# S5 input and output turned between channel order and (step, channel) order by DMA through DRAM instead of by quarter copies and column-strip products

## The chip, the cores and the metric

The kernel runs on one core of one Trainium2 chip. The metric is the device time of one execution in microseconds (us), lower is better. TensorE is called PE here, VectorE DVE, ScalarE ACT, GpSimd POOL and SyncE SP, as in the profile.

## What is computed

One decoder layer on a sequence of 512 steps and 1024 channels: a SwiGLU FFN, a token mixer, a second SwiGLU FFN, each with modulation from a vector c, a scaled residual and a LayerNorm. The mixer projects its input once; one half of the result feeds a Mamba-2 (SSD) head group, the other 512 channels, `u`, an S5 head group, and one output projection joins both. The S5 half is what the change touches:

```python
def s5_mixer(u, ...):
    uf = u.reshape(bsz, s_len, S5_GROUPS, S5_GROUP_CH)          # 32 groups of 16 channels
    bu_re = einsum('bsgh,gph->bsgp', uf, bb_re)                 # 64 complex states per group
    bu_im = einsum('bsgh,gph->bsgp', uf, bb_im)
    _, _, xr, xi = lax.associative_scan(combine, (a_seq_re, a_seq_im, bu_re, bu_im), axis=1)
    y = (einsum('bsgp,ghp->bsgh', xr, c_re) - einsum('bsgp,ghp->bsgh', xi, c_im) + uf * d)
    g = gelu(y)
    out = g * sigmoid(g @ w_glu + b_glu)
```

## The kernel before

The whole layer is written as one program. A scheduling layer takes the instructions in the order in which the code issues them and sets each engine's order from its own costs; an engine then runs its own list strictly in order, and a semaphore wait at its head holds all behind it. Large matrix products are done in three passes (high by high, high by low, low by high: lines 103, 104 and 105, `mm3`), so each weight tile is cast to a high part on ACT (`whi`, line 96) and its low part is subtracted on DVE (`wlo`, line 81).

The S5 half works on four blocks b of 128 channels. The scan runs over 128 groups of four steps: a column of the operand U holds four consecutive steps of 32 channels in its 128 partitions, that is (step, channel) order, and four such operands (r = 0 to 3) make a block. The input projection delivers channel order: 128 channels in the partitions, 512 steps along them. So the data has to be turned twice, before the scan and after it.

- `s5_u` (lines 930 to 940) turns the input: `u()` runs a projection of 24 matmuls, then 16 copies of 32 partitions x 128 steps from PSUM into U, 12 of them on ACT (line 938) and 4 on DVE (line 940).
- `s5_scan` (line 942) multiplies U by two matrices (line 949, 8 products per block), and on DVE rotates the result by E (line 81), scans its real and imaginary part (line 960) and rotates back into two tiles `s5X` (line 81 again). `s5_load` (line 927) loads the matrices of a block, `s5M`, from a DRAM buffer that an earlier phase filled.
- `s5_y` (line 970) multiplies U and the two X by three more matrices (line 978): 48 products per block, each 32 columns wide, four of them side by side in the four column strips, which write channel order straight into PSUM; one ACT copy (line 980) moves it to G.
- `s5_glu` (line 983) applies Gelu in place (line 993), splits G into a high and a low part (`ghl`) and multiplies by w_glu.

`mixer` (line 1247) issues these steps mixed with the conv projections of the SSD half, `conv`, also 24 matmuls each followed by ACT line 1111, three DVE passes of line 90 (`cv`) and a Silu (line 1115). The order is u(0), u(1), scan(0), u(2), scan(1), u(3), conv(4), y(0), conv(6), scan(2), conv(5), conv(7), y(1), conv(0), scan(3), y(2), conv(1), conv(2), y(3), the first part of the glu, conv(3), then the SSD scores (lines 1123 to 1134). The scheduler may shift them against one another. Every scan gets X tiles of its own from a pool with one buffer, so a scan's first X write waits until the y before it has read.

Of the kernel before, what the change touches and what calls it, by code (L numbers as in the profile page):

```python
# [10 lines left out]
F32 = mybir.dt.float32  # L11
# [3 lines left out]
AF = mybir.ActivationFunctionType  # L15
# [35 lines left out]
class Layer:  # L51
# [875 lines left out]
        self.nc.sync.dma_start(out=M, in_=self.s5_dram[b][:, k0:k0 + n])  # L927
        return M

    def s5_u(self, U, ups):  # L930

        nc = self.nc
        uv = ups.rearrange("p (t i) -> p i t", i=4)
        for r in range(4):
            for ii in range(4):
                o, a = U[32 * ii:32 * ii + 32, r, :], uv[32 * r:32 * r + 32, ii, :]
                if (r + ii) % 4 < 3:
                    nc.scalar.copy(out=o, in_=a)
                else:
                    nc.vector.tensor_copy(o, a)  # L940

    def s5_scan(self, sp, b, M, U):

        nc = self.nc
        w = []
        for n in range(2):
            ps = self.bank([P, 4, P])
            for r in range(4):
                nc.tensor.matmul(ps[:, r, :], M[:, n, r, :], U[:, r, :], start=True, stop=True)  # L949
            w.append(ps)  # L950
        mk = lambda n: sp.tile([P, 4, P], F32, tag="s5" + n, bufs=1, name=self.nm("s5" + n))
        d0, vr, vi = mk("d0"), mk("vr"), mk("vi")
        t = self.tmp.tile([P, 512], F32, tag="t2", name=self.nm("s5t")).rearrange("p (r t) -> p r t", r=4)
        nc.scalar.copy(out=d0, in_=bc(self.s5_m4[:, 4 * b:4 * b + 4], (2, P)))
        nc.gpsimd.memset(d0[:, :, 0:1], 0.0)
        Er, Ei = M[:, 2], M[:, 3]
        self.cmul(vr, vi, Er, Ei, w[0], w[1], None, t, conj=True)
# [3 lines left out]
        X = [sp.tile([P, 4, P], F32, tag=f"s5X{n}", bufs=1, name=self.nm("s5X")) for n in range(2)]  # L961
        for x in X:
            nc.gpsimd.memset(x[:, :, 0:1], 0.0)
        s = slice(0, P - 1)
        self.cmul(X[0][:, :, 1:], X[1][:, :, 1:], Er[:, :, s], Ei[:, :, s], vr[:, :, s], vi[:, :, s],
                  None, t[:, :, s])
        return X

    def s5_y(self, M, U, X, G):


        nc = self.nc
        ps = self.bank()
        pv = ps.rearrange("p (t j) -> p j t", j=4)
        for j in range(4):
            for n, rhs in enumerate((U, X[0], X[1])):
                for r in range(4):
                    nc.tensor.matmul(pv[32 * r:32 * r + 32, j, :], M[:, n, r, 32 * j:32 * j + 32],  # L978
                                     rhs[:, r, :], start=(n == 0), stop=(n == 2))
        return nc.scalar.copy(out=G, in_=ps).ins  # L980

    def s5_glu(self, G, mixT, after):


        nc = self.nc
        gl = []

        def split(k):
            gl.append(self.tmp.tile([P, 2, S], F32R, tag="t4", name=self.nm("ghl")))
            self.split(G[k], gl[k][:, 0, :], gl[k][:, 1, :])  # L990
        with self.tc.issue_after(after):
            for k in range(4):
                nc.scalar.activation(G[k], G[k], AF.Gelu_apprx_tanh)
        split(0), split(1)
# [253 lines left out]
    def mixer(self, hT, hp, job, finish):  # L1248
# [3 lines left out]
        with ExitStack() as ctx:  # L1252
# [33 lines left out]
            with tc.tile_pool(name="s5", bufs=1, reuse_waits="tile") as sp:  # L1286
# [5 lines left out]

                def u():
                    U.append(Ub[len(U)])
                    self.s5_u(U[-1], proj())

                def scan():
                    b = len(X)
# [1 line left out]
                    load(0)  # L1300

                def y(b):
                    i = self.s5_y(M[1][b], U[b], X[b], G[b])
                    load(1)
                    return i
                load(0), load(0), load(1), load(1)
# [17 lines left out]
                conv(1)  # L1324
                conv(2)
                mixT = []
                glu = self.s5_glu(G, mixT, y(3))
# [103 lines left out]
def body(tc, ins, out):  # L1431
# [3 lines left out]
    with ExitStack() as ctx:  # L1435
# [89 lines left out]
        L.pin = False  # L1525
        L.setup_cols()
        L.s5_m4 = L.cp.tile([P, 16], F32, name="s5m4")
        L.s5_dram = [tc.dram_tile([P, 7, 4, P], F32, name=f"s5d{b}") for b in range(4)]
        gp = gctx.enter_context(tile_pool("g1"))
        L.accp = gp  # L1530
# [118 lines left out]
```

## Time and profile before

| | |
|---|---|
| median of 3 runs | 968.11 us (967.95 to 968.97) |
| the profiled execution, its own time | 968.27 us |
| its span, first to last instruction | 966.6 us |
| PE, busy share of the span | 98% |
| DVE | 78% |
| ACT | 46% |
| DMA, mean over the span | 153 GB/s |

The profile is of one execution, and 1.7 us of its time lie outside its span. Busy time says how long an engine had an instruction in flight; matmuls are pipelined, one 512-column matmul shows 0.39 us but the next starts 0.227 us later. The granted TensorE clock is given as a share of 2.4 GHz: 1.00 is 2.4, 0.50 is 1.2.

### The profile page before, as it was taken

What the parts mean: (1) busy time and instruction counts of PE and PEld (TensorE: products, weight loads), DVE (VectorE), ACT (ScalarE), POOL (GpSimd) and SP (SyncE); (2) the same over time, 40 slices, a digit from 0 to 9 for tenths busy, and PEclk for the clock granted to TensorE, in tenths of its full rate; (3) what the DMA queues carried; (4) which work ended last, traced back from release to release, by engine and by line L of the source; (5) the groups of instructions that cost most, each with busy time, mean ns of one, the idle gap of its engine ahead of it and who ended that gap; (6) DMA issues with size and microseconds to landing.
All of it is one profiled execution on the core that took longest, in us unless ns stands there. A gap on an engine that the chain in (4) does not pass through costs nothing.

```text
span 966.6 us, 14710 instructions
## 1 busy us (share of the span) xinstructions
PE 944.9 (98%) x5409; PEld 798.1 (83%) x5409; DVE 758.4 (78%) x1522; ACT 446.9 (46%) x879; POOL 34.2 (4%) x73
## 2 busy tenths in 40 slices
PE   8999999999999999999999999999999999999996
PEld 5778888887877888778877777988999999988885
DVE  6579998963677888858995889785788888896947
ACT  3343452635443335545537844533455554633420
POOL 0000000000000000100000110100000000000003
PEclk9999999999999999999999999999999999999999
DMA  9968584453866766362432024532233232543302
GB/s 342 377 190 270 188 280 162 157 174 122 261 204 197 242 217 180 86 233 71 142 121 67 1 88 152 173 111 66 88 99 120 89 129 90 175 152 109 109 1 87
DMA packets 75578, 147.93 MB, mean 153 GB/s; under 512 B 11633, under 2 KB 28657, under 8 KB 74993
## 3 DMA queue, kind: packets, MB, share of 16 engines
q1 hardware_dynamic: 75216, 146.94, 46.1%
q8 instruction: 42, 0.69, 0.3%
q14 instruction: 32, 0.25, 0.1%
q10 hardware_dynamic: 288, 0.04, 0.0%
HBM read 137.52 MB, written 9.44 MB: 152 GB/s over the span
## 4 chain that ended last, share of the span: by engine, by line
PE 86%; DVE 6%; ACT 4%; issue 2%; POOL 1%; DMA 0%; DVEq 0%; POOLq 0%; ACTq 0%
PE ps L103 27%; PE ps L104 27%; PE ps L105 27%; DVE cv L90 1%; PE ps L253 1%; PE ps L978 1%; DVE wlo L81 1%; PE ps L207 1%; ACT whi L96 1%; POOL rsx L170 1%; DVE s5X L81 0%; DMA raw<-in_w_in_dram 0%; PE ps L295 0%; DVE s5t L81 0%; PE ps L949 0%
## 5 line engine op out<-in xcount | busy, mean ns | idle before, releaser
L96 ACT CAST whi<-raw 128x1024 fp32r<-128x1024 f32 (+1 forms) x155 | 155.0, 1007 | 211.5 <-PE ps L104 97.5
L81 DVE TENSOR_TENSOR wlo<-raw,whi 128x1024 fp32r<-128x1024 f32 (+1 forms) x155 | 179.3, 1167 | 43.0 <-ACT whi L96 42.5
L103 PE MATMUL ps<-hT,whi 128*128 128x512 f32 x448 | 177.0, 396 | 1.7 <-ACT hT L1492 1.7
L104 PE MATMUL ps<-hT,whi 128*128 128x512 f32 x448 | 174.7, 390 | 0.1
L105 PE MATMUL ps<-hT,wlo 128*128 128x512 f32 x448 | 174.6, 390 | 0.0
L103 PE MATMUL ps<-whi,ghl 128*128 128x512 f32 x320 | 125.2, 391 | 0.0
L104 PE MATMUL ps<-wlo,ghl 128*128 128x512 f32 x320 | 124.5, 389 | 0.0
L105 PE MATMUL ps<-whi,ghl 128*128 128x512 f32 x320 | 124.3, 389 | 0.0
L103 PEld LDWEIGHTS ps<-hT,whi 128*128 128x128 f32 x448 | 83.9, 188 | 23.3 <-issue 3.2
L105 PEld LDWEIGHTS ps<-hT,wlo 128*128 128x128 f32 x448 | 84.1, 188 | 17.8
L104 PEld LDWEIGHTS ps<-hT,whi 128*128 128x128 f32 x448 | 84.2, 188 | 17.0 <-DVE hT L81 0.5
L103 PE MATMUL ps<-hx,whi 128*128 128x256 f32 (+1 forms) x320 | 97.5, 305 | 0.7 <-DVE cp L90 0.6
L104 PE MATMUL ps<-hx,whi 128*128 128x256 f32 (+1 forms) x320 | 97.3, 304 | 0.0
L105 PE MATMUL ps<-hx,wlo 128*128 128x256 f32 (+1 forms) x320 | 97.3, 304 | 0.0
L90 DVE SCALAR_TENSOR_TENSOR acc<-ra,cs,acc 128x1024 f32<-128x1024 f32 (+2 forms) x62 | 71.0, 1145 | 22.4 <-DMA ra<-in_w_ada_dram 21.9
L96 ACT CAST ghl<-g 128x512 fp32r<-128x512 f32 x88 | 53.1, 619 | 50.1 <-PE ps L105 37.5
L103 PEld LDWEIGHTS ps<-whi,ghl 128*128 128x128 f32 x320 | 60.1, 188 | 14.6 <-issue 2.5
L105 PEld LDWEIGHTS ps<-whi,ghl 128*128 128x128 f32 x320 | 60.1, 188 | 12.6
L104 PEld LDWEIGHTS ps<-wlo,ghl 128*128 128x128 f32 x320 | 60.1, 188 | 12.3
L81 DVE TENSOR_TENSOR ghl<-g,ghl 128x512 fp32r<-128x512 f32 x88 | 58.1, 686 | 13.6 <-ACT ghl L96 13.6
L103 PEld LDWEIGHTS ps<-hx,whi 128*128 128x128 f32 x320 | 61.1, 191 | 3.9 <-issue 0.8
L104 PEld LDWEIGHTS ps<-hx,whi 128*128 128x128 f32 x320 | 61.2, 191 | 2.6
(474 smaller groups left out, 1693.0 us busy)
## 6 DMA issues: line engine op xcount, KB each, us to landing
ra<-in_w_ada_dram SPq DMA_DIRECT2D x56, 512.0 KB, 4.5
raw<-in_up_dram SPq DMA_DIRECT2D x49, 512.0 KB, 4.2
raw<-in_ffn_w_dram SPq DMA_DIRECT2D x44, 512.0 KB, 4.4
raw<-in_up_dram SPq DMA_DIRECT2D x64, 256.0 KB, 3.8
ra<-in_ada_dram SPq DMA_DIRECT2D x16, 512.0 KB, 7.8
raw<-in_w_in_dram SPq DMA_DIRECT2D x16, 512.0 KB, 4.4
s5d<-s5mp SPq DMA_DIRECT2D x20, 256.0 KB, 3.8
s5M<-s5d SPq DMA_DIRECT2D x4, 1024.0 KB, 5.1
```

Source lines behind the costliest of these rows:

```text
L81: self.nc.vector.tensor_tensor(out=out, in0=a, in1=b, op=op)
L90: self.nc.vector.scalar_tensor_tensor(out=out, in0=a, scalar=s, in1=b, op0=op0, op1=op1, **k)
L96: keep(self.nc.scalar.copy(out=hi, in_=src))
L103: mm(o, lh, rh, start=first, stop=False, **k)
L104: mm(o, lh, rl, start=False, stop=False, **k)
L105: self.last_mm = mm(o, ll, rh, start=False, stop=last, **k)
L170: self.nc.gpsimd.tensor_scalar(out=x, in0=var, scalar1=EPS, scalar2=None, op0=ADD)
L207: self.nc.tensor.matmul(ps, self.onesr, bc(self.onesr, (1, 4)), start=True, stop=True)
L253: nc.tensor.matmul(bank[q:q + 32, 0:256], lhs, w[:, :, m * P:(m + 1) * P], start=(j < 2), stop=(j >= len(put) - 2))
L978: nc.tensor.matmul(pv[32 * r:32 * r + 32, j, :], M[:, n, r, 32 * j:32 * j + 32], rhs[:, r, :], start=(n == 0), stop=(n == 2))
```

## The change

It turns both ways by DMA. `s5_turn` takes a channel-order tile of 128 partitions, issues four writes of 64 KB each into a DRAM buffer on ACT's DMA queue, in 512-byte pieces that land in (step, channel) order or back, and then one read of the whole 256 KB on POOL's queue. The input takes one ACT copy from PSUM and one turn. The output is now 12 full-width products per block in (step, channel) order, one ACT copy, and one turn whose result overwrites the block's U; Gelu reads that and writes G with a stride. The two X tiles and the decay row d0 are allocated and their first columns cleared once, for all four scans; the ACT copy of a scan fills the rest of d0.

```diff
+    def s5_turn(self, b, n, src, out):
+        d = self.s5_turns[b][:, n]
         for r in range(4):
-            for ii in range(4):
-                o, a = U[32 * ii:32 * ii + 32, r, :], uv[32 * r:32 * r + 32, ii, :]
-                if (r + ii) % 4 < 3:
-                    nc.scalar.copy(out=o, in_=a)
-                else:
-                    nc.vector.tensor_copy(o, a)
+            self.nc.scalar.dma_start(out=d[:, r].rearrange("(j c) t -> c j t", j=4), in_=src[32 * r:32 * r + 32])
+        self.nc.gpsimd.dma_start(out=out, in_=d)
+    def s5_u(self, b, U, ups):
+        c = self.tmp.tile([P, 1024], F32, tag="t4", ...)[:, :512].rearrange("p (j t) -> p j t", j=4)
+        self.nc.scalar.copy(out=c, in_=ups.rearrange("p (t i) -> p i t", i=4))
+        self.s5_turn(b, 0, c, U)
...
-        d0, vr, vi = mk("d0"), mk("vr"), mk("vi")
+        if b == 0:
+            self.s5_d0, *self.s5_x = mk("d0"), mk("X0"), mk("X1")
+            for a in (self.s5_d0, *self.s5_x):
+                nc.gpsimd.memset(a[:, :, 0:1], 0.0)
+        d0, X = self.s5_d0, self.s5_x
-        nc.scalar.copy(out=d0, in_=bc(self.s5_m4[:, 4 * b:4 * b + 4], (2, P)))
-        nc.gpsimd.memset(d0[:, :, 0:1], 0.0)
+        nc.scalar.copy(out=d0[:, :, 1:], in_=bc(self.s5_m4[:, 4 * b:4 * b + 4], (2, P - 1)))
-        X = [sp.tile([P, 4, P], F32, tag=f"s5X{n}", bufs=1, ...) for n in range(2)]
-        for x in X:
-            nc.gpsimd.memset(x[:, :, 0:1], 0.0)
...
+    def s5_y(self, b, M, U, X, G):
-        for j in range(4):
+        for r in range(4):
             for n, rhs in enumerate((U, X[0], X[1])):
-                for r in range(4):
-                    nc.tensor.matmul(pv[32 * r:32 * r + 32, j, :], M[:, n, r, 32 * j:32 * j + 32],
-                                     rhs[:, r, :], start=(n == 0), stop=(n == 2))
-        return nc.scalar.copy(out=G, in_=ps).ins
+                nc.tensor.matmul(ps[:, r, :], M[:, n, r, :], rhs[:, r, :], start=(n == 0), stop=(n == 2))
+        c = self.tmp.tile([P, 1024], F32, tag="t4", ...)[:, :512].rearrange("p (j t) -> p j t", j=4)
+        i = nc.scalar.copy(out=c, in_=ps).ins
+        self.s5_turn(b, 1, c, G)
+        return i
+    def s5_glu(self, T, G, mixT, after):
-                nc.scalar.activation(G[k], G[k], AF.Gelu_apprx_tanh)
+                nc.scalar.activation(G[k].rearrange("p (t j) -> p j t", j=4), T[k], AF.Gelu_apprx_tanh)
```

Three places show how the engines' lists move. The changed file has two lines more from line 930 on, so its line 977 is the product of line 978, its 950 that of 949, its 1116 that of 1115.

The first is PE's list at y(0). `ps_4627` is its bank, `zx` holds U, `s5X_4418` and `s5X_4419` are the X of block 0; the X of block 1 are two other tiles. Before:

```order
L1080 MATMUL ps_4618<-ident,nacs 32x128
L978 MATMUL ps_4627<-zx_4225,s5M_4233 32x128 x4
L978 MATMUL ps_4627<-s5X_4418,s5M_4233 32x128 x4
L978 MATMUL ps_4627<-s5X_4419,s5M_4233 32x128 x4
L978 MATMUL ps_4627<-zx_4225,s5M_4233 32x128 x4
```

Now, with one pair of X tiles for all blocks:

```order
L977 MATMUL ps_4589<-zx_4229,s5M_4237 128x128
L977 MATMUL ps_4589<-s5X_4391,s5M_4237 128x128
L103 MATMUL ps_4617<-hT_2999,whi_4342 128x512
L977 MATMUL ps_4589<-s5X_4392,s5M_4237 128x128
L977 MATMUL ps_4589<-zx_4229,s5M_4237 128x128
```

The code issues y(0) behind scan(1), and as both now name the tiles s5X_4391 and s5X_4392, y(0) takes them as scan(1) leaves them; in the same way y(1) stands behind scan(2), and y(2) and y(3) behind scan(3). In the list of before, y(0) waits for scan(0) alone.

The second is PE's list from scan(3) on. `ps_4837` is the bank of y(2), `ps_4931` that of y(3), `ps_4809` and `ps_4814` those of scan(3). Before, all of y(2) followed scan(3) at once. Now:

```order
L950 MATMUL ps_4809<-zx_4229,s5M_4494 128x128 x4
L950 MATMUL ps_4814<-zx_4229,s5M_4494 128x128 x4
L977 MATMUL ps_4837<-zx_4229,s5M_4609 128x128
...
L977 MATMUL ps_4837<-s5X_4391,s5M_4609 128x128
...
L977 MATMUL ps_4931<-zx_4229,s5M_4770 128x128
L977 MATMUL ps_4931<-s5X_4391,s5M_4770 128x128
...
L977 MATMUL ps_4837<-s5X_4392,s5M_4609 128x128
L977 MATMUL ps_4837<-zx_4229,s5M_4609 128x128
L977 MATMUL ps_4837<-s5X_4391,s5M_4609 128x128
L977 MATMUL ps_4837<-s5X_4392,s5M_4609 128x128
```

The first gap holds 44 matmuls of conv(1) and conv(2), the second and third four each, of conv(2) and conv(3); the rest of y(2) and then of y(3) follow without a gap, and 20 matmuls of conv(3) behind them.

The third is ACT's list from y(2) to the glu. `s5c_4850` and `s5c_4944` are the copies of y(2) and y(3), `s5t` the DRAM buffers, `zx_4229` holds the turned blocks, `zx_4226` G. Before, the list read (the copy of y(2), line 980, stands further ahead):

```order
L980 COPY zx_4222<-ps_5071 128x512
L993 ACT_TABLE_LOAD
L993 ACTIVATE zx_4222<-zx_4222 128x512
L1115 ACT_TABLE_LOAD
L1115 ACTIVATE zx_4223<-cv_5065 128x512
L993 ACT_TABLE_LOAD
L993 ACTIVATE zx_4222<-zx_4222 128x512 x3
```

Now:

```order
L979 COPY s5c_4850<-ps_4837 128x512
L934 DMA s5t_645<-s5c_4850 32x4x128 x4
L1116 ACTIVATE zx_4227<-cv_4925 128x512
L979 COPY s5c_4944<-ps_4931 128x512
L994 ACT_TABLE_LOAD
L994 ACTIVATE zx_4226<-zx_4229 128x4x128
L934 DMA s5t_646<-s5c_4944 32x4x128 x4
L994 ACTIVATE zx_4226<-zx_4229 128x4x128 x2
L96 CAST ghl_4955<-zx_4226 128x512
```

Two table loads are gone; eight DMA issues stand ahead of the first `ghl`, and so does the Gelu of block 2, which needs that block's turn.

## Rows read from the trace of the kernel before

**Rows 1.** The page's busy time of two engines: busy us, share of the span, instructions.
```profile
PE 944.9 (98%) x5409; PEld 798.1 (83%) x5409; DVE 758.4 (78%) x1522; ACT 446.9 (46%) x879; POOL 34.2 (4%) x73
```

**Rows 2.** Busy time in two stretches of 20 us in the S5 stage; the columns are the stretch, its length, then busy time and instructions of PE, its weight loads, DVE, ACT and POOL, the granted PE clock, the DMA engines' busy share and GB/s.
```profile
440.00:460.00 20.00, 20.00 (x108) 17.21 (x107) 19.30 (x38) 11.18 (x35) 0.10 (x1) 1.00 0.25 79
...
480.00:500.00 20.00, 17.68 (x244) 14.99 (x244) 20.00 (x28) 8.37 (x12) 0.38 (x5) 0.91 0.42 145
```

**Rows 3.** PE in order of time around y(0) and y(2): start, us, line, operation, in brackets the idle time before it and what ended it. A block's y has 96 records (48 products in two passes each).
```profile
460.83 0.43 PE L978 MATMUL ps<-zx,s5M 128*32 128x128 f32 x8
463.59 0.50 PE L103 MATMUL ps<-hT,whi 128*128 128x512 f32 x1
...
492.82 0.43 PE L978 MATMUL ps<-s5X,s5M 128*32 128x128 f32 x8 [0.24 <-DVE s5X L81]
495.33 0.65 PE L978 MATMUL ps<-s5X,s5M 128*32 128x128 f32 x8 [2.08 <-DVE s5X L81]
...
499.23 0.50 PE L103 MATMUL ps<-hT,whi 128*128 128x512 f32 x1
```

**Rows 4.** A stretch of 1 us right behind that wait, in the columns of rows 2.
```profile
496.00:497.00 1.00, 1.00 (x24) 1.00 (x20) 1.00 (x2) 1.00 (x2) 0.00 (x0) 0.50 0.51 195
```

**Rows 5.** PE in order of time at two other places with waits.
```profile
397.51 0.50 PE L103 MATMUL ps<-zw,hT 128*128 128x512 f32 x1 [0.74 <-ACT hT L96]
...
399.39 0.62 PE L105 MATMUL ps<-zw,hT 128*128 128x512 f32 x1 [1.14 <-DVE hT L81]
...
434.33 0.41 PE L1029 MATMUL ps<-ident,dtfm 16*128 16x16 f32 x4 [0.80 <-ACT dtfm L1026]
```

**Rows 6.** DVE in order of time: one input copy of 16; then without a gap a weight split, a product, the scan and another product; the first product of scan(2); a conv pass and the last X write of scan(3).
```profile
443.64 0.28 DVE L940 COPY zx<-ps 32x128 f32<-32x128 f32 x1
...
457.94 1.22 DVE L81 TENSOR_TENSOR wlo<-raw,whi 128x1024 fp32r<-128x1024 f32 x1
459.07 0.68 DVE L81 TENSOR_TENSOR s5t<-s5M,ps 128x512 f32<-128x512 f32 x1
459.67 1.22 DVE L960 TENSOR_TENSOR_SCAN s5vr<-s5d,s5vr 128x512 f32<-128x512 f32 x1
460.81 0.67 DVE L81 TENSOR_TENSOR s5vi<-s5vi,s5t 128x512 f32<-128x512 f32 x1
...
475.96 0.67 DVE L81 TENSOR_TENSOR s5vr<-s5M,ps 128x512 f32<-128x512 f32 x1
...
508.96 0.74 DVE L90 SCALAR_TENSOR_TENSOR cv<-ps,cols,cv 128x511 f32<-128x511 f32 x1
509.62 0.68 DVE L81 TENSOR_TENSOR s5X<-s5X,s5t 128x508 f32<-128x508 f32 x1
```

**Rows 7.** PE in order of time: the products of scan(0), the conv or projection matmul behind them, the products of scan(1).
```profile
440.26 1.95 PE L949 MATMUL ps<-zx,s5M 128*128 128x128 f32 x16
441.96 0.48 PE L103 MATMUL ps<-hT,whi 128*128 128x512 f32 x1
...
447.86 2.03 PE L949 MATMUL ps<-zx,s5M 128*128 128x128 f32 x16
```

**Rows 8.** ACT in order of time: the first input copies of block 0 and of block 1.
```profile
430.58 0.78 ACT L938 COPY zx<-ps 32x128 f32<-32x128 f32 x3
...
441.30 0.79 ACT L938 COPY zx<-ps 32x128 f32<-32x128 f32 x3
```

**Rows 9.** The second of the two issues that ACT's DMA queue had, at the start of the program: start, us, line.
```profile
1.22 0.46 ACTq L188 DMA_DIRECT2D b_ada<-in_badaT_dram  x1
```

**Rows 10.** DMA issues of 256 KB on SP's queue, the first kind out of DRAM, the second into it: count, KB each, median us from issue to landing.
```profile
raw<-in_up_dram SPq DMA_DIRECT2D x64, 256.0 KB, 3.8
...
s5d<-Er SPq DMA_DIRECT2D x4, 256.0 KB, 2.5
```

**Rows 11.** The spread over all transfers into and out of the S5 buffer in DRAM.
```profile
DMA to landing us min/median/max: 2.0/4.2/10.6
```

**Rows 12.** Two stretches in which the first turn would run, in the columns of rows 2.
```profile
430.00:432.00 2.00, 2.00 (x11) 0.77 (x9) 1.26 (x2) 1.34 (x4) 0.00 (x0) 1.00 1.01 422
...
436.00:438.00 2.00, 2.00 (x11) 1.65 (x10) 0.26 (x2) 1.65 (x3) 0.00 (x0) 1.00 0.01 2
```

**Rows 13.** ACT in order of time, from the copy of y(3) to the first split of the glu.
```profile
513.24 0.59 ACT L980 COPY zx<-ps 128x512 f32<-128x512 f32 x1
513.85 1.28 ACT L993 ACT_TABLE_LOAD   x1
515.14 0.63 ACT L993 ACTIVATE zx<-zx 128x512 f32<-128x512 f32 x1
...
520.59 1.12 ACT L96 CAST ghl<-zx 128x512 fp32r<-128x512 f32 x2
```

**Rows 14.** PE in order of time: y(3), the last matmul of conv(3), the SSD scores, the glu.
```profile
510.35 0.42 PE L978 MATMUL ps<-zx,s5M 128*32 128x128 f32 x8
...
518.45 0.39 PE L105 MATMUL ps<-hT,wlo 128*128 128x512 f32 x1
518.68 0.38 PE L1123 MATMUL ps<-zx 128*128 128x128 f32 x2
...
521.25 1.21 PE L103 MATMUL ps<-ghl,whi 128*128 128x512 f32 x4 [0.35 <-ACT ghl L96]
```

**Rows 15.** A stretch of 40 us behind the glu, in the columns of rows 2.
```profile
560.00:600.00 40.00, 37.32 (x180) 30.33 (x181) 34.86 (x53) 17.04 (x38) 3.96 (x8) 1.00 0.39 134
```

More of the change, by code (lines that the diff above doesn't have):

```diff
@@ L928, in s5_load @@
         return M
-    def s5_u(self, U, ups):
-        nc = self.nc
-        uv = ups.rearrange("p (t i) -> p i t", i=4)
+    def s5_turn(self, b, n, src, out):
+        d = self.s5_turns[b][:, n]
         for r in range(4):
-            for ii in range(4):
-                o, a = U[32 * ii:32 * ii + 32, r, :], uv[32 * r:32 * r + 32, ii, :]
-                if (r + ii) % 4 < 3:
-                    nc.scalar.copy(out=o, in_=a)
-                else:
-                    nc.vector.tensor_copy(o, a)
+            self.nc.scalar.dma_start(out=d[:, r].rearrange("(j c) t -> c j t", j=4), in_=src[32 * r:32 * r + 32])
+        self.nc.gpsimd.dma_start(out=out, in_=d)
+    def s5_u(self, b, U, ups):
+        c = self.tmp.tile([P, 1024], F32, tag="t4", name=self.nm("s5c"))[:, :512].rearrange("p (j t) -> p j t", j=4)
+        self.nc.scalar.copy(out=c, in_=ups.rearrange("p (t i) -> p i t", i=4))
+        self.s5_turn(b, 0, c, U)
     def s5_scan(self, sp, b, M, U):
@@ L951, in s5_scan @@
         mk = lambda n: sp.tile([P, 4, P], F32, tag="s5" + n, bufs=1, name=self.nm("s5" + n))
-        d0, vr, vi = mk("d0"), mk("vr"), mk("vi")
+        if b == 0:
[3 more added lines that the diff above has]
+        d0, X = self.s5_d0, self.s5_x
+        vr, vi = mk("vr"), mk("vi")
         t = self.tmp.tile([P, 512], F32, tag="t2", name=self.nm("s5t")).rearrange("p (r t) -> p r t", r=4)
-        nc.scalar.copy(out=d0, in_=bc(self.s5_m4[:, 4 * b:4 * b + 4], (2, P)))
-        nc.gpsimd.memset(d0[:, :, 0:1], 0.0)
+        nc.scalar.copy(out=d0[:, :, 1:], in_=bc(self.s5_m4[:, 4 * b:4 * b + 4], (2, P - 1)))
         Er, Ei = M[:, 2], M[:, 3]
@@ L960, in s5_scan @@
             nc.vector.tensor_tensor_scan(out=fl(v), data0=fl(d0), data1=fl(v), initial=0.0, op0=MUL, op1=ADD)
-        X = [sp.tile([P, 4, P], F32, tag=f"s5X{n}", bufs=1, name=self.nm("s5X")) for n in range(2)]
-        for x in X:
-            nc.gpsimd.memset(x[:, :, 0:1], 0.0)
         s = slice(0, P - 1)
@@ L967, in s5_scan @@
         return X
-    def s5_y(self, M, U, X, G):
+    def s5_y(self, b, M, U, X, G):
         nc = self.nc
-        ps = self.bank()
-        pv = ps.rearrange("p (t j) -> p j t", j=4)
-        for j in range(4):
+        ps = self.bank([P, 4, P])
+        for r in range(4):
             for n, rhs in enumerate((U, X[0], X[1])):
-                for r in range(4):
-                    nc.tensor.matmul(pv[32 * r:32 * r + 32, j, :], M[:, n, r, 32 * j:32 * j + 32],
-                                     rhs[:, r, :], start=(n == 0), stop=(n == 2))
-        return nc.scalar.copy(out=G, in_=ps).ins
-    def s5_glu(self, G, mixT, after):
+                nc.tensor.matmul(ps[:, r, :], M[:, n, r, :], rhs[:, r, :], start=(n == 0), stop=(n == 2))
+        c = self.tmp.tile([P, 1024], F32, tag="t4", name=self.nm("s5c"))[:, :512].rearrange("p (j t) -> p j t", j=4)
+        i = nc.scalar.copy(out=c, in_=ps).ins
+        self.s5_turn(b, 1, c, G)
+        return i
+    def s5_glu(self, T, G, mixT, after):
         nc = self.nc
@@ L1294, in u @@
                     U.append(Ub[len(U)])
-                    self.s5_u(U[-1], proj())
+                    self.s5_u(len(U) - 1, U[-1], proj())
                 def scan():
@@ L1302, in y @@
                 def y(b):
-                    i = self.s5_y(M[1][b], U[b], X[b], G[b])
+                    i = self.s5_y(b, M[1][b], U[b], X[b], U[b])
                     load(1)
@@ L1326, in mixer @@
                 mixT = []
-                glu = self.s5_glu(G, mixT, y(3))
+                glu = self.s5_glu(U, G, mixT, y(3))
                 next(glu)
@@ L1527, in body @@
         L.s5_m4 = L.cp.tile([P, 16], F32, name="s5m4")
+        L.s5_turns = [tc.dram_tile([P, 2, 4, P], F32, name=f"s5t{b}") for b in range(4)]
         L.s5_dram = [tc.dram_tile([P, 7, 4, P], F32, name=f"s5d{b}") for b in range(4)]
```

## The prediction, made blind

> **What bounds the kernel now.** I read the page's busy table first: PE is busy 98% of the span [rows 1], so the change can move the end only by what it does to PE's own work and to PE's waits. Then the table by stage. In the S5 stage DVE is nearly as full as PE, 19.3 and 20.0 of 20 us in two of its stretches [rows 2]: it is DVE's list that PE waits for. PE in order of time shows the one large wait. At y(2) PE stands 0.24 and then 2.08 us for DVE's last X writes, and behind that the granted clock is 0.50, the lower level of 1.2 GHz [rows 3, 4]. The 80 records from 495.33 to 499.23 take 3.9 us; y(0) does 96 in 2.76 us, so 80 are worth 2.3, and 1.6 us went to the clock. This place costs 2.3 + 1.6 = 3.9 us. A second, smaller wait of 0.35 us stands before the glu [rows 14].
>
> The clock has a second witness: waits of 0.74 and 1.14 us, two matmuls between them, are followed by matmuls of 0.62 instead of 0.39 us, while one wait of 0.80 us leaves the next ones alone [rows 5].
>
> **The change, part by part.** *Copies.* 48 small ACT copies and 16 on DVE go. On DVE one takes 0.28 us [rows 6] and some 0.32 with the gap behind it; eleven of them stand between the first product of scan(0) and the last X write at 510.3, 3.5 us of a full engine.
>
> *Products of y.* The 16 records of scan(0) take 441.96 - 440.26 = 1.70 us at full width [rows 7]. The 24 full-width records of a y take 1.5 times that, 2.55 us, against 2.76 [rows 3]. That is 0.2 us a block, 0.8 at most in four.
>
> *The turn of the input.* ACT's copy of 128x512 takes 0.59 us [rows 13] and starts where the copies started, 430.58 and 441.30 [rows 8]. Four issues follow at 0.46 us [rows 9], so the last begins 0.6 + 3 x 0.46 = 2.0 us after the copy's start. A 256 KB write into DRAM lands in 2.5 us and a read of 256 KB in 3.8 [rows 10]; no issue of POOL's queue is in the trace, and I take the read's row for it. That is 2.0 + 2.5 + 3.8 = 8.3 us a turn. The bounds are 2.0 us for each half, the fastest transfer, and 10.6 for a half in full engines, the slowest [rows 11]: 6.0 to some 15 us. With 8.3 us U(0) is there at 438.9, or a little later, since the engines are full with the `s5M` loads at 431 (share 1.01) [rows 12]; PE wants it at 440.26 [rows 7]. U(1) is there at 449.6 and PE wants it at 447.86 [rows 7]: a new wait of 1.7 us. U(2) and U(3) have 10 us and more to spare. Behind the four issues, from 433.0 on, ACT has the copy `dtfm`, which PE waits for up to 434.33 as it is [rows 5]; I cost that at nothing.
>
> On this a rule speaks against the change. The Trainium skill, DMA: Bandwidth & Descriptors, section Anatomy of one DMA, says that a DMA costs about 2 us however small it is, most of it for the confirmation that the last byte has landed, worst when the target is HBM. By it, with 0.6 us for the 256 KB at its 436 GB/s, an estimate for a turn is 2.0 + 2.0 + 2.6 = 6.6 us, and U(1) would be there at 447.9 with no wait; the rows say 8.3, and this trace has no pair of dependent transfers to decide it.
>
> *The new wait of y(0).* It now reads X as scan(1) leaves it, so it waits for DVE's whole list up to there. DVE's `wlo` follows the cast that ACT ends at 441.3, when its copies begin [rows 8], and takes 1.13 us [rows 6]. From there the list of the changed kernel holds 24 products of scan(0) and scan(1) at 0.60 us start to start, four scans of 1.14, two splits of 1.13 and a short `dec` of 0.1 [rows 6]. That is 442.5 + 14.4 + 4.6 + 2.3 + 0.1 = 463.9; with some gaps where a product needs the one before, 464.2. U(0) may be 0.9 us late for PE, and U(1) 3.0 us, before this list moves. PE comes to y(0) at 460.8 [rows 3], or at 462.5 after a wait for U(1). So PE loses about 3 us between 447 and 464, in one portion or two. Ten products are left after 464.2, 2.1 us: y(0) ends at 466.4. If the clock drops as it did at y(2), 1.6 us more, 468.0. Before, y(0) and the one matmul that now stands inside it ended at 463.8. So PE is 2.6 to 4.2 us late here.
>
> *Where that goes.* Scan(2) follows 22 matmuls later; its first bank is ready 5.0 + 1.0 us after y(0), at 472.4 to 474.0, and DVE, which has one `bd`, three conv passes, three short ones and a split in between, some 6.5 us, is free by 470.7 and starts it then instead of at 475.96 [rows 6]. ACT's casts of `csel` hold its second product, as they do before; I allow them up to 0.9 us in the early case. From there DVE's list is as long as before, 34.3 us to the last X write at 510.3 [rows 6]. It ends at 507.5 to 508.5, 1.8 to 2.8 us sooner. PE meets y(1) without a wait of weight, and y(2) no longer stalls: only its first product stands behind scan(3), the rest after 44 matmuls. The 3.9 us of rows 3 and 4 are what pays for the wait at y(0).
>
> *The end of the stage.* Call the last X write T. Before, PE starts y(3) at T and the glu at 521.25, T + 10.9 [rows 14]. Now 19 products of y(2) and y(3), 4.05 us, 20 matmuls of 0.23 [rows 14], 4.55, and the scores, 521.25 - 0.35 - 518.68 = 2.2 [rows 14], make T + 10.8. But ACT's list is longer: its Silu of conv(2) waits for DVE's two splits of 1.13 and four conv passes of 0.66 [rows 6], to T + 5.0; then Silu 0.65, copy 0.65, table load 1.3, Gelu 0.65, four issues 1.8, two Gelus 1.3, split 0.55 [rows 9, 13]: T + 11.9. So the glu begins 1.0 us after PE is ready. The turn of y(2) (copy at T + 2.3, 8.3 us) lands at T + 10.6, just where its Gelu stands; each us more is a us of delay. POOL holds its read behind two clears that wait for y(3), to T + 5.3, which is earlier than the writes land.
>
> *Sum.* 2.8 or 1.8 sooner at T, less 1.0 at the glu: 1.8 or 0.8 us gained. After the glu PE has 2.7 us of waits between 560 and 600 [rows 15], and I let them stand. I take 1.0 us, the middle less a little for a late turn. Against its own 968.27 that is 967.3; the runs' median is 968.11, 0.2 lower, so the forecast is 967.1.
>
> **Rivals.** *Faster: the waits stay short.* If the turn takes 6 to 7 us and PE's 3 us of waiting are split between scan(1) and y(0) with work between, the clock stays up (0.80 us alone did not drop it, rows 5), T is at 507.5, the Gelus come sooner, and the two saved table loads shorten ACT's list behind the glu. Then the gain is up to 2.8: 965.3 to 966.1. Against it: the two cases that did drop the clock had 1.9 and 2.3 us of waiting, and here are about 3.
>
> *Slower: the turn is on the path.* U(0) is needed on DVE by 441.2 and U(1) by 450.9. Beyond that, DVE's list up to y(0) moves one for one, and the turn of y(2) delays the glu one for one as well. The point is a turn of about 9.5 to 10 us. At 13 us (a read of 8.5, between the median and the slowest) U(0) comes 2.4 us late for DVE and U(1) 3.4, and the turn of y(2) costs 4.7 at the glu: 968.1 - 1.0 + 3.4 + 4.7 = 975 at worst, 970 to 972 for 11 us. For it: POOL's queue is unmeasured, 512-byte pieces are small, and the engines are full at 431. Against it: they are empty from 436 and the median rows give 8.3.
>
> *Nothing moves.* The copies were hidden on ACT, half idle, and what DVE saves is eaten by the later X that y(0) reads: within 0.2% with another cause than mine, the same time.
>
> **From cases to numbers.** 0.2% (1.9 us) is about what a measurement of this kernel tells from no change. The forecast, with a gain or a loss below it, 0.5 including the last rival; the faster rival 0.26; the slower one 0.24. The range leaves out half of the outer two: 965.2 to 970.9. The forecast's own range is 966.2 to 969.
>
> **What would show it.** Right: an idle entry of 1 to 2 us before the products of scan(1), ended by a DMA; PE waiting for s5X at y(0) and, with the first, some 3 us in all; no wait at y(1) and y(2); a wait of about 1 us for `ghl` at the glu; DVE some 4.5 us less busy, ACT some 13. Wrong: a turn above 10 us or below 7 from the copy's start to the read's landing; the granted clock at 1.00 all through the S5 stage (then the gain is larger); a Gelu of block 2 waiting for its DMA; PE's waits after the glu grown or shrunk by more than 1 us.

## The result: slower by half a per cent

| | before | changed |
|---|---|---|
| median of 6 runs | 968.03 us (966.54 to 968.97) | 973.91 us (971.29 to 975.56) |
| ratio, 95% interval | | 1.0055, 1.0039 to 1.0071 |
| profiled execution, own time and span | 968.27, 966.6 | 971.4, 969.7 |

The forecast was 967.1 us in a range of 965.2 to 970.9. The change is 5.9 us slower, outside that range, and clear of 0.2%.

The page of the changed kernel, answering to [rows 1]. DVE has 5.7 us less work and ACT 10.6 us less, as the change promises; PE is no busier. The loss is in PE's waits.

```profile
PE 942.5 (97%) x5121; PEld 796.8 (82%) x5121; DVE 752.7 (78%) x1506; ACT 436.3 (45%) x833; POOL 36.0 (4%) x72
```

PE of the changed kernel in order of time, the rows with a wait from 430 to 522, in the columns of [rows 3] (they answer to [rows 3, 5, 7, 14]):

```profile
431.96 0.42 PE L1030 MATMUL ps<-ident,dtfm 16*128 16x16 f32 x4 [0.67 <-ACT dtfm L1027]
439.88 2.05 PE L950 MATMUL ps<-zx,s5M 128*128 128x128 f32 x16 [1.84 <-DMA zx<-s5t]
448.06 2.02 PE L950 MATMUL ps<-zx,s5M 128*128 128x128 f32 x16 [0.27 <-PE ps L1062]
462.01 0.46 PE L977 MATMUL ps<-s5X,s5M 128*128 128x128 f32 x2 [0.65 <-DVE s5X L81]
463.45 0.46 PE L977 MATMUL ps<-s5X,s5M 128*128 128x128 f32 x2 [0.76 <-DVE s5X L81]
504.40 0.49 PE L977 MATMUL ps<-s5X,s5M 128*128 128x128 f32 x2 [0.36 <-DVE s5X L81]
521.19 1.94 PE L103 MATMUL ps<-ghl,whi 128*128 128x512 f32 x4 [2.89 <-ACT ghl L96]
```

The stall at y(2) is gone, as forecast. New are 1.84 us for the turn of block 0 at scan(0), 1.41 us at y(0), and 2.89 us at the glu. The clock fell there too, where [rows 4] show it at y(2):

```profile
522.00:524.00 2.00, 2.00 (x6) 1.54 (x5) 2.00 (x4) 2.00 (x3) 0.00 (x0) 0.50 0.00 0
```

Where the time went can be cut at matmuls that both profiles have: the `dtfm` transposes, the first product of the glu, and the first and the last product of the second FFN's first tiles (`hx,wg`).

| stretch, us | before | changed | difference |
|---|---|---|---|
| start to the `dtfm` transposes | 434.33 | 431.96 | -2.37 |
| to the glu | 86.92 | 89.23 | +2.31 |
| to the first `hx,wg` | 84.52 | 86.73 | +2.21 |
| to the last `hx,wg` | 25.42 | 26.26 | +0.84 |
| to the end of the span | 335.36 | 335.48 | +0.12 |

The first line is not the change's doing. Before, the clock falls behind the waits at 397 to 399 [rows 5]; in this execution the waits are there (0.58 and 1.15 us) and the clock stayed up, which is worth 1.7 of the 2.37 us. The other 0.65 us lies ahead of 397, where the profiles scatter by a microsecond with the change and without it. Of the 14 profiles of this study it fell at that place in 5, among them kernels with the change and without it. Without this luck the profiled loss is 5.5 us, about that of the medians.

### The profile page after: what moved, and what is told of

It reads as the page before. It is cut to its first block, busy times and chain, and to the rows that moved or that the text cites. A ratio compares the mean times of both kernels' runs of the same rounds, so it can differ in the third digit from the quotient of the medians.

```text
span 969.7 us, 14129 instructions
## 1 busy us (share of the span) xinstructions
PE 942.5 (97%) x5121; PEld 796.8 (82%) x5121; DVE 752.7 (78%) x1506; ACT 436.3 (45%) x833; POOL 36.0 (4%) x72
## 4 chain that ended last, share of the span: by engine, by line
PE 85%; DVE 8%; issue 2%; DMA 2%; POOL 1%; ACT 1%; ACTq 0%; POOLq 0%; DVEq 0%
PE ps L103 27%; PE ps L104 26%; PE ps L105 26%; DMA s5t<-s5c 1%; PE ps L977 1%; PE ps L253 1%; DVE s5t L81 1%; DMA zx<-s5t 1%; PE ps L207 1%; DVE wlo L81 1%; DVE s5X L81 1%; DVE res L87 1%; POOL rsx L170 1%; PE ps L950 0%; DVE st L672 0%
## 5 line engine op out<-in xcount | busy, mean ns | idle before, releaser
L103 PEld LDWEIGHTS ps<-hx,whi 128*128 128x128 f32 x320 | 61.1, 191 | 3.9 <-issue 0.8
L105 PEld LDWEIGHTS ps<-hx,wlo 128*128 128x128 f32 x320 | 61.2, 191 | 2.5
```

The lines of the kernel that those rows point to most:

```text
L103: mm(o, lh, rh, start=first, stop=False, **k)
L105: self.last_mm = mm(o, ll, rh, start=False, stop=last, **k)
```

## Experiments

All times are medians, and each ratio is against runs of the kernel before beside it on the same chip (967.2 to 968.24 us).

### The same kernel again

> The changed kernel a second time, for a second profile and more times. The first six executions lie between 971.3 and 975.6 while the profiled one is at 971.4. Theory A (the turn is slower than 8.3 us because its writes queue behind weight loads, which makes PE wait at scan(0), y(0) and the glu; whether the granted clock falls at each of these waits differs from execution to execution and makes the spread): median 972 to 975, the same waits within 0.5 us, about 1.8 at scan(0), 1.4 at y(0), 2.9 at the glu, and other drops of the clock than in the first profile if the time is other. Rival (the waits themselves differ from execution to execution, since transfers meet other transfers): the turns' lengths differ by more than 1.5 us between the two profiles.

972.69 us, ratio 1.0050 (1.0035 to 1.0064). The same waits within 0.1 us, but for the glu: there 3.59 instead of 2.89 us, and the lower clock lasted 6.8 us instead of 3.4. The Gelu of block 2 shows why. First the changed kernel, then its second execution, ACT in order of time:

```profile
519.61 1.10 ACT L994 ACTIVATE zx<-zx 128x512 f32<-128x512 f32 x1 [3.22 <-DMA zx<-s5t]
520.51 0.62 ACT L96 CAST ghl<-zx 128x512 fp32r<-128x512 f32 x1
```

```profile
520.13 1.10 ACT L994 ACTIVATE zx<-zx 128x512 f32<-128x512 f32 x1 [3.92 <-DMA zx<-s5t]
521.03 0.62 ACT L96 CAST ghl<-zx 128x512 fp32r<-128x512 f32 x1
```

Counted from the `dtfm` transposes (431.96 and 431.83), this Gelu began 0.65 us later and the glu (521.19 and 521.71) also 0.65 us later: the turn of y(2) is on the path, one for one. By its own bound of 1.5 us the rival of the expectation fails here: between the two profiles no turn differs by more than 0.7 us. But what there is of it counts at this place, and gelu_out, below, shows an execution in which the waits themselves are others.

### One direction alone

Input only: `s5_turn` and the new `s5_u`, the rest as before. Output only: the new `s5_y` and Gelu, the 16 input copies as before. Both keep X tiles of their own for each scan.

```text
 input only                                   output only
 new:    s5_turn, s5_u by copy and turn       new:    s5_turn, s5_y full width, one copy and turn
 before: s5_y in column strips, one copy      new:    Gelu reads the turned block, writes G with a stride
 before: Gelu in place                        before: s5_u by 16 copies
```

> Only the input is turned by DMA; the output's column-strip products, its single copy and the X tiles of their own are as before, and PE's list is the same as before. Theory A: PE waits 1 to 2 us at the products of scan(0) for the turn; DVE's list is shorter by the input copies, so the stall of 2.3 us at y(2) and the clock's fall behind it go; the glu follows T by 10.9 as before. 964.5 to 967.5. Rival B (the pair of X tiles shared by all scans costs the time): the input turn costs nothing, and this kernel gains at least as much, also below 967. Rival C (what is lost is lost behind the glu, by another order of the engines' lists from there on): this kernel loses 1 us or more between 540 and 640.

> Only the output is turned by DMA; the 16 input copies and X tiles of their own are as before. Theory A: the stall at y(2) and its clock stay (T at about 510), and the glu comes late by the four issues, the slower strided Gelu and the splits behind them: PE waits 2.5 to 3.5 us for ghl at the glu, and the clock falls there in most executions. 970.5 to 974. Rival B (the shared X): 966.5 to 968.5, as the kernel before. Rival C: the loss lies behind the glu.

Input only: 965.61 us, ratio 0.9980 (0.9968 to 0.9993), a gain. Output only: 972.09 us, ratio 1.0045 (1.0030 to 1.0060). The times are those of theory A; that of input only would fit rival B as well, which the waits below refute. PE of the input-only kernel, its first products of scan(0), scan(1) and the glu:

```profile
440.79 0.38 PE L950 MATMUL ps<-zx,s5M 128*128 128x128 f32 x1 [0.50 <-DMA zx<-s5t]
...
450.19 1.02 PE L950 MATMUL ps<-zx,s5M 128*128 128x128 f32 x7 [1.51 <-issue]
...
519.26 0.97 PE L103 MATMUL ps<-ghl,whi 128*128 128x512 f32 x3 [0.35 <-ACT ghl L96]
```

The profile names no releaser for the 1.51 us, but the read of U(1) landed at 450.10. So the kernel pays 2.0 us for late turns at the two first scans, the larger part at the second, but between them and the glu PE never waits: the 3.9 us of [rows 3, 4] are gone. The output-only kernel keeps the stall at y(2) (2.02 us) and waits 1.26 us at the glu, half of what theory A had, so its time came out by another way than that theory's; it reaches the glu when the kernel before does, and its whole loss lies behind the glu, as rival C said (the table further below).

### X tiles of their own, and two pairs

The first undoes the sharing as it was before; the second keeps one clearing but alternates between two pairs of X.

```diff
 own_x:  s5_scan as before (X and d0 allocated and cleared for every scan)
 two_x:
-            self.s5_d0, *self.s5_x = mk("d0"), mk("X0"), mk("X1")
+            self.s5_d0, *self.s5_x = mk("d0"), mk("X0"), mk("X1"), *self.s5_g    # two blocks of G
-        d0, X = self.s5_d0, self.s5_x
+        d0, X = self.s5_d0, self.s5_x[2 * (b % 2):2 * (b % 2) + 2]
```

> Both turns by DMA, but every scan has X tiles and a d0 of its own, as before. Theory A: no wait at y(0), the wait at scan(0) stays, y(2) stalls less than 0.5 us, the wait of about 3 us at the glu stays: 968.5 to 972, only 2 to 4 us below the changed kernel. Rival B (the shared X tiles are what costs): 967.5 or less.

> The changed kernel with a second pair of X tiles (in the two G blocks that are not yet in use), scans 0 and 2 on one pair, 1 and 3 on the other, each cleared once; PE's list in the S5 stage is the one of before again. Theory A2 (the changed kernel loses in three places: the shared X, which makes PE wait 1.4 us at y(0) and puts y(2) behind scan(3), so that its turn is late for the Gelu; the longer list of ACT at the glu; another order of all engines behind the glu): no wait at y(0), the wait of 1.8 us at scan(0) stays, y(2) does not stall or by less than 1 us, the wait at the glu falls from 2.9 to between 1 and 2 us, and 2 to 4 us are still lost behind the glu. 967 to 970. Rival B (the shared X is all that costs): 966 or less. Rival D (the shared X costs nothing, own_x was no slower for another reason): 972 to 974.

own_x: 973.13 us, ratio 1.0056 (1.0035 to 1.0076), above theory A's range. A wait took the place of the one removed. POOL's read of y(0) waits at the head of POOL's list for the writes, and behind it stand the mask `cselt`, and the clearing of the next X. POOL, then DVE:

```profile
474.58 0.55 POOL L935 DMA_DIRECT2D zx<-s5t  x1 [8.79 <-DMA s5t<-s5c]
475.13 1.34 POOL L1075 TENSOR_SCALAR_AFFINE_SELECT cselt<-cselt 32x512 f32<-32x512 f32 x2
...
479.11 0.69 DVE L81 TENSOR_TENSOR s5t<-s5M,ps 128x512 f32<-128x512 f32 x1 [5.55 <-ACT csel L1078]
```

DVE, the full engine, loses 5.55 us, and PE waits for X at y(2) and y(3), 4.1 us in all, of which 2.8 are at y(2), where theory A had less than 0.5; at the glu it waits 1.49 us and not about 3. So this run does not isolate the sharing.

two_x does: its POOL list has the mask (466.09) ahead of the read (472.25). 970.32 us, ratio 1.0031 (1.0018 to 1.0044), 0.3 us above theory A2's range. PE, the first products of scan(0), of the glu, and a product of the second FFN:

```profile
440.18 1.05 PE L950 MATMUL ps<-zx,s5M 128*128 128x128 f32 x7 [1.71 <-DMA zx<-s5t]
...
517.26 0.50 PE L103 MATMUL ps<-ghl,whi 128*128 128x512 f32 x1 [1.28 <-ACT ghl L96]
...
621.73 0.39 PE L104 MATMUL ps<-hx,wg 128*128 128x256 f32 x1 [1.55 <-DVE hx L81]
```

No wait at y(0), none at y(2), and 1.28 us at the glu, where the changed kernel has 2.89. From the `dtfm` transposes to the glu it takes 84.88 us against 89.23: sharing one pair of X, with the order of the lists that follows from it, cost the changed kernel 4.3 us in this stage. Yet two_x, 2.0 us ahead of the kernel before at the glu, ends behind it. What it loses comes later.

### Behind the glu: three lists, three lengths

From the glu on, the lists of PE, DVE, ACT and POOL are the same, but for shapes and line numbers, within before's group (the first three rows), within the changed kernel's (the next two, where turn_read differs in the first dozen rows) and within the last row; between the groups 32 to 52 of DVE's 488 rows and 22 to 34 of ACT's 367 stand elsewhere, and 47 to 64 of PE's 2682. Each figure is the difference of two start times in one profile.

| kernels | `dtfm` to glu | glu to first `hx,wg` | first to last `hx,wg` |
|---|---|---|---|
| before | 86.92 | 84.52 | 25.42 |
| in_only, collide | 85.05, 86.72 | 84.49, 84.48 | 25.45, 25.44 |
| mix_dma, mix_act, act_123 | 84.09, 84.09, 82.60 | 84.50, 84.44, 84.48 | 25.42, 25.44, 25.45 |
| changed, again | 89.23, 89.88 | 86.73, 88.04 | 26.26, 26.24 |
| gelu_read, gelu_out, turn_read | 88.83, 88.88, 87.16 | 86.70, 86.68, 86.50 | 26.25, 26.27, 26.26 |
| two_x, own_x, out_only | 84.88, 89.98, 86.84 | 86.62, 86.56, 87.64 | 27.06, 27.17, 27.01 |

Every kernel that turns the output has other lists from the glu on, and these are 1.6 us (last group) or 0.8 us (the group of the changed kernel) longer in the last column, a hundred us behind the change, to within 0.2 us whatever happened before. In the middle column two_x, own_x and turn_read lose 2.0 to 2.1 us with the clock at 1.00 throughout; changed, gelu_read, gelu_out and out_only have one fall of the clock in it, again a longer one. What the fall is worth there cannot be told apart: turn_read, with nearly the lists of the changed kernel and the clock up, waits more and loses almost as much. What this looks like is seen at the 1.55 us of two_x. DVE of two_x, then of the kernel before:

```profile
617.93 0.42 DVE L81 TENSOR_TENSOR hx<-tf,hx 128x256 fp32r<-128x256 f32 x1
620.05 1.28 DVE L90 SCALAR_TENSOR_TENSOR acc<-ra,cs,acc 128x1024 f32<-128x1024 f32 x1 [1.70 <-DMA ra<-in_w_ada_dram]
621.25 0.42 DVE L81 TENSOR_TENSOR hx<-tf,hx 128x256 fp32r<-128x256 f32 x1
```

```profile
620.51 0.98 DVE L81 TENSOR_TENSOR hx<-tf,hx 128x256 fp32r<-128x256 f32 x2
624.20 2.60 DVE L90 SCALAR_TENSOR_TENSOR acc<-ra,cs,acc 128x1024 f32<-128x1024 f32 x2 [2.71 <-DMA ra<-in_w_ada_dram]
```

In two_x an accumulation for the next modulation that waits for its weights stands ahead of the last `hx`; in the kernel before the last `hx` come first. In the last column this order explains the last group: two_x, own_x and out_only wait 1.5 to 1.7 us there for that last `hx`. The changed kernel waits 0.54 and 0.58 us for two other `hx`, the kernel before 0.30 for one, which makes up its 0.84 us. For the middle column the lists are argued from the grouping alone: a kernel with the output turn and the lists of before was not run.

### What a turn costs

In the changed kernel the eight turns take 11.5, 9.2, 10.5 and 8.3 us (input), 9.6, 11.0, 10.1 and 7.8 us (output), from the start of ACT's copy to the landing of the read. The four writes of the input turns of blocks 0 and 2 and of y(1), from issue to landing, in this order, and the DMA engines' share (last but one column) in the stretches in which they were in flight:

```profile
DMA to landing us min/median/max: 5.3/5.4/5.6
...
DMA to landing us min/median/max: 1.7/1.8/1.8
...
DMA to landing us min/median/max: 4.9/5.6/5.8
```

```profile
430.00:434.00 4.00, 3.33 (x17) 2.10 (x16) 1.15 (x6) 2.09 (x3) 0.00 (x0) 1.00 1.00 358
449.00:452.00 3.00, 3.00 (x19) 2.62 (x19) 3.00 (x5) 0.70 (x2) 0.00 (x0) 1.00 0.32 87
490.00:495.00 5.00, 5.00 (x32) 4.45 (x31) 3.38 (x6) 2.34 (x3) 0.00 (x0) 1.00 1.03 357
```

To test this, `collide` adds traffic to the input-only kernel just where block 2's writes met none:

```diff
+        for m in range(6 if b == 2 else 0):
+            self.nc.sync.dma_start(out=self.s5_idle[:, m], in_=c)
```

> The kernel with only the input turned by DMA, and in addition SP's queue writes the copy of block 2 six times, 1.5 MB, into a DRAM buffer that nobody reads; the first four of these writes start when the four writes of block 2's turn start. The lists of PE, DVE, ACT and POOL are unchanged. Without them the four writes of block 2 landed 1.3 us after their last issue, while those of blocks 0 and 1, with weight loads in flight, took 3.4 to 5.2 us. Theory (a turn's writes queue behind whatever is in flight in the same 16 engines): they now land 3.5 to 5.5 us after the last issue. Rival (the difference has another cause: the block, its place in DRAM, the first use of the queue): 1.3 to 2 us as before. The time itself should not move by more than 1 us, block 2 has 10 us to spare.

965.95 us (one run). Block 2's writes in the input-only kernel, then in collide:

```profile
DMA to landing us min/median/max: 1.7/1.8/1.8
```

```profile
DMA to landing us min/median/max: 2.7/3.4/5.3
```

The last write landed 4.4 us after its issue had ended instead of 1.3, and that turn took 14.3 instead of 10.3 us. The theory holds: a turn's writes share the DMA engines with what other queues have in flight. Its time hides a loss: the clock stayed up at 399 here and fell there in the profile of input only. From the `dtfm` transposes to the glu collide took 86.72 us against 85.05; the turn of block 3 took 15.3 us instead of 11.1, and PE waited 0.33 and 0.85 us for X at y(2) and y(3), which the expectation did not have.

`turn_read` changes the number and the size of the pieces instead:

```diff
-        for r in range(4):
-            self.nc.scalar.dma_start(out=d[:, r].rearrange("(j c) t -> c j t", j=4), in_=src[32 * r:32 * r + 32])
-        self.nc.gpsimd.dma_start(out=out, in_=d)
+        self.nc.scalar.dma_start(out=d, in_=src)
+        for j in range(4):
+            self.nc.gpsimd.dma_start(out=out[32 * j:32 * j + 32], in_=d[:, j].rearrange("(r c) t -> c r t", r=4))
```

> The changed kernel with the turn's two halves exchanged: one write of 256 KB in pieces of 2 KB, one issue on ACT instead of four, and four reads of 64 KB in pieces of 512 bytes, four issues on POOL instead of one. Theory (queueing behind loads sets the length, not the number or the size of the pieces): writes with loads in flight still land 3 us or more after their issue, the turn of y(2) is again 9 to 11 us, ACT's list is 1.4 us shorter for each turn; 971 to 974. Rival (four issues and 512-byte pieces are what is slow): the turns fall to 7 to 8.5 us, the wait at the glu falls below 2 us, 969 to 971.

971.4 us, ratio 1.0036 (1.0026 to 1.0046). The write of block 2, with little in flight, landed 2.0 us after its issue; that of y(1), beside weight loads, 5.8:

```profile
DMA to landing us min/median/max: 2.0/2.0/2.0
...
DMA to landing us min/median/max: 5.8/5.8/5.8
```

So what is in flight sets the length of a write, not the number or the size of its pieces, and the turn of y(2) is 9.7 us, as the theory said. What ACT saves comes back on POOL, whose four issues take 2.2 us where one takes 0.55: the eight turns took 10.2 us in the mean. PE did not wait for U(0) and U(1). At U(1) the saved issues show, 7.2 us against 9.0 to 9.2 in every kernel with four; at U(0) they do not, 9.6 us against 9.8 in gelu_out, where the clock fell at 399 as it did here.

One sign of the rival was seen all the same: PE no longer waited 2.9 us at the glu. The cause is not a shorter turn. The lists of the S5 stage came out otherwise here, and ACT's has the first split of the glu ahead of the Gelu of block 2. ACT, then PE:

```profile
519.49 0.63 ACT L96 CAST ghl<-zx 128x512 fp32r<-128x512 f32 x1
...
523.25 1.11 ACT L994 ACTIVATE zx<-zx 128x512 f32<-128x512 f32 x1 [1.52 <-DMA zx<-s5t]
```

```profile
521.50 0.50 PE L103 MATMUL ps<-ghl,whi 128*128 128x512 f32 x1
...
524.84 0.96 PE L103 MATMUL ps<-ghl,whi 128*128 128x512 f32 x3 [0.30 <-ACT ghl L96]
```

The last X write ended at 510.85, and the glu began 10.65 us behind it (10.95 in the kernel before), 1.65 us ahead of the landing of the turn of y(2). So the turn of y(2) is on the path in the changed kernel because its Gelu stands ahead of the first split.

### Gelu

> The changed kernel, and Gelu walks through its block in the order of G: it reads with a stride and writes without one. PE's list is that of the changed kernel. Theory A2: the 1.1 us of a Gelu is its strided write, and it falls to about 0.65; the glu starts 0.4 to 0.6 us sooner behind the landing of the turn of y(2), and the median falls by 0.3 to 1.0 us, to 972 to 973. Rival: it is the pattern of three dimensions itself that is slow, and the Gelu stays at 1.1 us, the median where it is.

> The changed kernel, and Gelu reads its block with a stride and writes G without one (in the run gelu_read it did both with a stride, and took 1.12 us). Theory: the strided write is what makes a Gelu 1.1 us instead of 0.63; it falls to below 0.75, the glu starts about 0.45 us sooner behind the landing of the turn of y(2), the median falls by 0.3 to 1 us. Rival: it stays at 1.1 us, and so does the time.

```diff
-                nc.scalar.activation(G[k].rearrange("p (t j) -> p j t", j=4), T[k], AF.Gelu_apprx_tanh)
+                nc.scalar.activation(G[k].rearrange("p (t j) -> p t j", j=4), T[k].rearrange("p j t -> p t j"), ...)
```

Both runs had this one edit: Gelu reads with a stride and writes without. The second expectation describes the first run wrongly; it had no stride in its write either. The Gelu of gelu_read:

```profile
514.12 1.13 ACT L994 ACTIVATE zx<-zx 128x512 f32<-128x512 f32 x1
```

The rival holds as far as the time of a Gelu goes: 1.13 us, against 0.63 in [rows 13], with the stride on either side. That a pattern of three dimensions is slow by itself does not follow: ACT's copies of the input read PSUM in steps of 16 bytes and took 0.58 us. 971.27 us (1.0047, 1.0029 to 1.0065) and 974.08 us (1.0068, 1.0052 to 1.0083) are two series of one kernel on two chips. Their profiles have one fall of the clock ahead of the span's end, and three.

### Taking the copies from DVE without the output turn

mix_dma: the kernel before with the input turns of blocks 2 and 3 alone. mix_act: no DMA turn, ACT does all 16 copies of blocks 2 and 3. act_123: the same for blocks 1 to 3.

```diff
-    def s5_u(self, U, ups):
+    def s5_u(self, U, ups, b=0):
-                if (r + ii) % 4 < 3:
+                if b >= 2 or (r + ii) % 4 < 3:        # mix_act; act_123: b >= 1
```

> The kernel before with only the inputs of blocks 2 and 3 turned by DMA; blocks 0 and 1, which PE wants soon, keep their 16 copies, and the output is as before. PE's list is that of before. Theory A2: no waits at scan(0) and scan(1), where the kernel with all inputs turned by DMA lost 2.0 us; DVE's list is 8 copies or 2.6 us shorter, so y(2) stalls 0.5 us at most and the clock stays up there. 963 to 965.5. Rival (what the input turn gained came from the copies of blocks 0 and 1): 966 to 968.

> The kernel before, and the four copies of blocks 2 and 3 that DVE did are done by ACT; no DMA at all. Theory A2: what counts is the 2.6 us less on DVE, not the DMA; the stall at y(2) falls to 0.5 us at most and the clock stays up: 963 to 965.5, like the kernel whose blocks 2 and 3 go by DMA. Rival (the DMA itself, or ACT's emptier list, made the gain): 967 to 968.5.

> The kernel before, and the four copies that DVE did for blocks 1, 2 and 3 are done by ACT (in the run mix_act those of blocks 2 and 3). No DMA turns. Theory (DVE's list sets when the last X comes, PE waited 0.84 us for it at y(3) in mix_act): DVE's list is another 1.3 us shorter, that wait goes, and U(1) is still in time; 963.0 to 964.8, up to 0.8 us below mix_act. Rival: U(1) comes late for PE by the 1.1 us that ACT's 16 copies take longer, and the time is that of mix_act or 1 us more.

965.52 us (0.9976, 0.9966 to 0.9985), 964.66 us (0.9976, 0.9966 to 0.9986) and 963.32 us (0.9962, 0.9948 to 0.9975; 963.02 to 964.93). Theory A2 holds for all three, mix_dma at the edge of its range: the gain of the input turn was DVE's shorter list and not the DMA, which mix_act does not have. Without late turns it is larger in the profiles (84.09 us from the `dtfm` transposes to the glu, against 85.05 for input only); the intervals of the medians overlap. act_123, two stretches in the columns of [rows 2]:

```profile
480.00:500.00 20.00, 20.00 (x263) 17.04 (x263) 19.52 (x28) 8.02 (x12) 0.53 (x5) 1.00 0.36 120
500.00:520.00 20.00, 19.65 (x170) 15.52 (x170) 14.00 (x20) 13.60 (x19) 1.09 (x2) 1.00 0.16 54
```

The stall of [rows 3] is gone, the clock stays up, and the 0.35 us before the glu of [rows 14] are left. With 4.5 us less than the kernel before beside it, this is the lowest median here, though its interval overlaps those of the other two, and it has none of the change's DMA.

## Why the prediction was wrong

**The turn.** This step failed first. 8.3 us were forecast; eight turns took 7.8 to 11.5 us, 9.8 in the mean. Copy, issues and read were about right, but for one read of 6.2 us; the 0.3 to 0.7 us from the last landing of a write to the issue of the read were put at nothing. The writes were taken from the median of 2.5 us in [rows 10]. The four writes behind it took 2.0 us twice, with the DMA engines at 0.35, and 3.1 and 4.2 us with the engines at 0.94 and 0.61; [rows 12] showed the engines full just where the first turn was to run, and the text passed over it with "a little later". The Trainium skill, DMA: Bandwidth & Descriptors, section Issuing engines are not separate DMA queues, says that transfers from all engines end on the same 16 DMA engines and interleave; collide agrees (1.8 us in the median alone, 3.4 beside the added writes). The figure of about 2 us a DMA that the prediction took from the Trainium skill, DMA: Bandwidth & Descriptors, section Anatomy of one DMA, is given there for DMAs issued on POOL's queue, so it covers the reads alone; the turn of 6.6 us estimated from it is shorter than all eight. The undisturbed writes, on ACT's queue, come near it (1.7 to 1.8 us).

**The waits at the scans and y(0).** PE was to lose about 3 us there in one portion or two; it lost 3.5 (1.84, 0.27, 0.65, 0.76). Sum right, place not: U(0) and not U(1) was late. The clock did not fall. The place differs from execution to execution: in gelu_out, with the same lists up to there and with the clock's fall at 399 that [rows 5] have, PE waited 1.86 us at scan(1), near the 1.7 of the forecast, and not at scan(0) or y(0), and the clock fell behind it. The waits summed to 1.9 us there, so the sum of 3.5 in the changed kernel's profile came near the forecast in part by luck.

**T, the last X write.** Forecast 1.8 to 2.8 us sooner. Counted from the `dtfm` transposes it came at 74.9 us (506.86 - 431.96) against 76.0 (510.3 - 434.33), 1.1 us sooner: U(0) landed 3.3 us after the forecast time, and DVE's list began 1 us later for it. y(1) and y(2) did not stall, as forecast.

**The glu.** Forecast at T + 11.9, it began at T + 14.3. The turn of y(2) landed at T + 12.7 instead of T + 10.6, and a Gelu took 1.1 us where 0.65 was put in; turn_read shows that it was the Gelu's place ahead of the first split that put this turn on the path. The forecast had costed the new stride at nothing. Of this the Trainium skill, SBUF — State Buffer, section Door 1: The DMA port swizzle, has a rule that the prediction missed: accesses that leave a line of 16 bytes each time pay for it. Both strides here do, and both runs show 1.1 us; a shorter stride was not run. So PE waited 2.9 us at the glu, not 1.0, and behind such a wait the clock fell in all four profiles that had 2.7 us or more there.

**Behind the glu.** "I let them stand" was the other failed step. The lists from there on were never compared, and by the table the changed kernel lost 3.05 us there against before. 0.84 of it are waits for `hx`, with another list on DVE; the 2.2 us of the middle column are lists and clock together, and how much is whose stays open.

**Sum.** Forecast -1.0; measured +2.3 to the glu, +2.2 and +0.8 behind it, together 5.5 with 0.1 at the end. The slower rival had its mechanism right: the turn is on the path from 9.5 to 10 us on, and the turn of y(2) delays the glu one for one. It had 0.24, and no price for the lists. "Nothing moves" failed: DVE's copies did bind, as in_only and mix_act show.

**The signs listed.** Seen: PE waiting for s5X at y(0), none of weight at y(2), the Gelu of block 2 waiting for its DMA, four turns above 10 us, and PE's waits behind the glu grown by 1.5 us. Not seen: the wait of 1 to 2 us before scan(1); it was 0.27. The clock stayed at 1.00 up to the glu, but the larger gain that was to come with it did not. DVE lost 5.7 us of work, not 4.5, ACT 10.6 and not 13, of which the slower Gelus are 2.0.

**The medians.** The changed kernel scatters over 4 us, more than before's 2.4. The gelu pair shows the likely reason: one kernel, in whose two profiles the clock fell once and three times, 2.1 us apart in span. Each new wait of 1 to 3 us is one more place for it.

## What to carry to other kernels

A transfer through DRAM on a chain is priced with the load that other queues have in flight at that time, not by the median of its kind; and sharing a buffer to save clearing can tie a reader to a later writer. Work that does not need a late transfer belongs ahead of the work that waits for it, as ACT's list in turn_read shows. Before moving work off a full engine by DMA, try the idle engine that is already there: here 12 copies moved from DVE to ACT gained 4.5 us. After a change to a scheduled program, compare the lists of all engines to the end, since as much was lost behind the glu, up to a hundred us behind the change, as in the changed stage itself.

## What the runs showed of the hardware

The length of a wait does not tell whether the clock falls: behind 1.14 or 1.15 us (with 0.45 to 0.86 us just ahead) it fell in 5 of 14 profiles; behind 1.84 us at scan(0) it did not, behind 1.86 us at scan(1) in gelu_out it did; behind the 2.1 us at y(2) it fell in the kernel before, behind 2.05 us there in own_x it did not. Ahead of the last 10 us of the program a fall lasted 3.4 us in all but one case (6.8). A write of 64 KB into DRAM landed 1.7 to 1.8 us after its issue with little in flight, and up to 5.8 us beside weight loads in the changed kernel. A Gelu of 128x512 took 1.1 us instead of 0.63 with a stride on either side in SBUF, while a copy of this size that reads PSUM with a stride took 0.58.
